# Expert weights in 1 MB units for the first ten experts of each layer instead of the first five

## The chip, the cores and the metric

The kernel runs on one core of a Trainium2 chip. The time is device microseconds (us) of one execution. Five engines work side by side: PE (matrix products), DVE (vector), ACT (scalar), POOL and SP; SP's queue only issues DMA transfers here. Before the change three runs took 1260.52 to 1263.24 us, median 1263.21 us. The execution that was profiled took 1264.12 us.

## The reference

Two layers on 256 tokens of width 1024, in float32. Layer 0 mixes the tokens by forgetting attention (phase A), layer 1 by retention (phase C). After each mixer a router picks one of 4 groups for a token and 2 of its 8 experts, and each expert is a SwiGLU product:

```python
def expert_block(args):
    xb, e = args
    a, b = jnp.split(xb @ w_gu[e], 2, axis=-1)
    return (jax.nn.silu(a) * b) @ w_down[e]
...
h = x
for i in range(DEPTH):
    hn = rms_norm(h, norm_mix[i])
    h = h + mixer(hn)             # attention in layer 0, retention in layer 1
    hn = rms_norm(h, norm_ffn[i])
    h = h + hier_moe(hn, ...)     # 32 experts
return rms_norm(h, norm_final)
```

(`mixer` stands for the two calls.) All 32 experts of a layer get tokens, so all weights are read: an expert has `w_gu` of 1024 x 1024 (4 MB) and `w_down` of 512 x 1024 (2 MB), 192 MB in a layer.

## The kernel before, in words

**The order of work.** Phase A, the expert phase of layer 0, phase C, the expert phase of layer 1, the last norm. An expert phase goes through experts 0 to 31 in order, in groups of four. For an expert, PE multiplies its tokens with `w_gu` (`first_product`, line 1047), ACT and DVE make the SwiGLU product, DVE transposes it, and PE multiplies it with `w_down` (`expert`, line 1075). After the third expert of a group PE gathers the tokens of the next group (`gather`, line 970), after the fourth it scatters the results (line 1101). After the first group comes `overflow`, a loop under an `If` for experts with more than 32 tokens (line 1254); with these inputs it is jumped over, but every engine has to pass the branch in its own order.

**The weights.** All weights go through one list, `Stream.todo`, in the order in which PE uses them, into 26 units of SBUF of 1 MB each (`NSLOT`). A transfer of 1 MB takes one free unit, `one()`; a transfer of 2 MB takes a free pair of neighbours, units 2i and 2i + 1, `two()`. `done` gives units back when the last product that reads them has been written down, and `pump` then issues what is next in the list. `pump` never passes over an item: when the first item finds no pair, it stops there.

```python
            slot = self.one() if units == 1 else self.two()
            if slot is None:
                return
...
    def pieces(e):
        return 2 if e < FINE or e == NE - 1 else 1
```

`pieces` (line 282) tells how an expert is cut. With 1 piece there are three transfers of 2 MB, two for `w_gu` and one for `w_down`; with 2 pieces there are six of 1 MB. `first_product` and `expert` call `done` as soon as a transfer's own products are issued: after 8 matmuls of line 1047 for 1 MB of `w_gu` (16 in the profile), after 16 for 2 MB. `FINE` is thus the number of experts at the start of a layer that come in 1 MB units; expert 31 always does.

**Units that are not weights.** The work buffers take units from the same 26 (`claim`, `Room`): one for the router, two more that are claimed at expert 0, and two that `overflow` claims before its branch and gives back behind it. `reserve` keeps as many units free as are about to be claimed.

**The queue.** Every transfer of the list is issued by SP, in list order (line 166). A DMA waits until PE has read what was in its units. It also waits for the landing of the DMA eight places before it, since there are eight DMA semaphores in turn; so at most eight transfers are under way. Which units a transfer gets, and so which PE product it waits for, is decided when the program is built.

Of the kernel before, what the change touches and what calls it, by code (L numbers as in the profile page):

```python
# [28 lines left out]
CAP = 32  # L29
NSLOT = 26  # L30

FINE = 5
AHEAD = 3

WARM = 29
# [192 lines left out]
def trunk(ctx, tc, x, fox_w_in, fox_b_f, fox_w_out, ret_w_in, ret_gn_gain, ret_w_out,  # L228
# [53 lines left out]
    def pieces(e):  # L282
        return 2 if e < FINE or e == NE - 1 else 1

# [1292 lines left out]
```

## Time and profile before

| what | value |
|---|---|
| runs before | 1260.52, 1263.24, 1263.21 us; median 1263.21 us |
| the profiled execution | 1264.12 us; its span 1262.4 us |
| PE busy | 992.3 us, 79% of the span |
| DVE, ACT, POOL busy | 416.7, 317.0, 46.8 us |
| SP's DMA queue, share of 16 DMA engines | 90.0% |
| read from HBM | 459.70 MB, 365 GB/s over the span |
| mean granted TensorE clock | 0.915 of full speed |

Three views are used. The windows view gives the busy time of each engine and the DMA rate in a stretch; a stretch with a lower rate than its neighbours is one in which the DMA engines had nothing to do for part of the time. The timeline of SP tells when a transfer was issued, and what it cost on SP; the view of DMA issues tells how long after its issue it landed, so that the sum is its time of landing. The timeline of PE has in brackets how long PE stood before an instruction, and what ended that.

### The profile page before, as it was taken

How to read it: one execution, taken by the hardware profiler on the slowest of the kernel's cores; microseconds unless marked ns; L12 is line 12 of the kernel's file. 1: busy time of each engine (PE TensorE's matmuls, PEld its weight loads, DVE VectorE, ACT ScalarE, POOL GpSimd, SP SyncE). 2: the span in 40 equal slices, each digit the busy share in tenths (PEclk: the TensorE clock that was granted, in tenths of full speed). 3: DMA queues.
4: the chain of work that ended last, by engine and by line, in shares of the span. 5: the costliest groups of instructions: out<-in, count | busy, mean ns of one | idle time of the engine just before them, and what ended most of it. 6: DMA issues, size and time to landing. Idle time of an engine off the chain costs nothing. (4 is left out here: it accounts for less than half of the span.)

```text
span 1262.4 us, 21607 instructions
## 1 busy us (share of the span) xinstructions
PE 992.3 (79%) x9279; PEld 638.7 (51%) x9279; DVE 416.7 (33%) x931; ACT 317.0 (25%) x670; POOL 46.8 (4%) x55
## 2 busy tenths in 40 slices
PE   8999986777576666678999999977766666676787
PEld 8888853343232333234989888743432333233344
DVE  6776741211111111112777776421111111111113
ACT  5665521111010010101554665311110101010111
POOL 2000000000000000000223100000000000000001
PEclk9999999999797979789999999999978787877879
DMA  9966878999999999999982678779999999999994
GB/s 327 336 253 228 307 295 342 429 424 428 427 427 427 428 427 426 428 428 393 371 318 77 242 258 336 276 295 421 427 427 426 427 428 428 426 428 426 428 424 175
DMA packets 70088, 462.22 MB, mean 366 GB/s; under 512 B 8401, under 2 KB 13281, under 8 KB 41570
## 3 DMA queue, kind: packets, MB, share of 16 engines
q1 hardware_dynamic: 69568, 460.70, 90.0%
q8 instruction: 75, 1.23, 0.4%
q14 instruction: 27, 0.22, 0.0%
q10 hardware_dynamic: 418, 0.07, 0.0%
HBM read 459.70 MB, written 1.05 MB: 365 GB/s over the span
## 5 line engine op out<-in xcount | busy, mean ns | idle before, releaser
L1047 PE MATMUL sc<-slot,slot 128*32 128x256 f32 x4096 | 281.2, 426 | 57.5 <-DMA slot<-in_expert_w_gu_dram 54.2
L1047 PEld LDWEIGHTS sc<-slot,slot 128*32 128x32 f32 x4096 | 137.8, 120 | 188.4 <-issue 81.3
L1075 PE MATMUL o<-slot,slot 128*32 128x256 f32 x1984 | 145.5, 441 | 105.3 <-DMA slot<-in_expert_w_down_dram 59.6
L1075 PEld LDWEIGHTS o<-slot,slot 128*32 128x32 f32 x1984 | 72.5, 123 | 173.6 <-issue 85.6
L1057 DVE TENSOR_TENSOR slot<-slot,sc 128x128 f32<-128x128 f32 x64 | 23.8, 371 | 396.6 <-ACT slot L1056 396.6
L467 DVE SCALAR_TENSOR_TENSOR slot<-slot,gT,slot 128x512 fp32r<-128x512 f32 x160 | 125.0, 801 | 50.0 <-ACT slot L456 48.6
L500 PE MATMUL acc<-slot,slot 128*128 128x256 f32 x960 | 125.1, 287 | 0.9 <-ACT slot L456 0.4
L1090 DVE COPY slot<-o 32x256 f32<-32x256 f32 x124 | 51.8, 418 | 215.4 <-PE o L1075 188.2
L456 ACT ACTIVATE slot<-slot,gT 128x512 fp32r<-128x512 f32 x160 | 111.4, 718 | 36.2 <-PE acc L500 15.1
L500 PEld LDWEIGHTS acc<-slot,slot 128*128 128x128 f32 x960 | 118.6, 192 | 3.3 <-ACT slot L456 0.7
L1088 ACT ACTIVATE slot<-o 32x256 f32<-32x256 f32 x124 | 46.5, 375 | 292.6 <-DVE slot L1090 292.6
L1056 ACT ACTIVATE slot<-sc 128x128 f32<-128x128 f32 x64 | 17.7, 277 | 383.9 <-PE sc L1047 383.9
L512 PE MATMUL acc<-slot,slot 128*128 128x512 f32 x256 | 102.5, 400 | 0.0
L513 PE MATMUL acc<-slot,slot 128*128 128x512 f32 x256 | 100.1, 391 | 1.8 <-DVE slot L467 1.8
L514 PE MATMUL acc<-slot,slot 128*128 128x512 f32 x256 | 100.1, 391 | 0.0
L970 PE MATMUL sc<-h,slot 128*128 128x512 f32 x112 | 69.3, 778 | 33.5 <-DVE slot L959 33.5
L1101 PE MATMUL acc<-slot,slot 128*128 128x512 f32 (+1 forms) x128 | 60.9, 611 | 13.2 <-ACT slot L1088 13.2
L970 PEld LDWEIGHTS sc<-h,slot 128*128 128x128 f32 x112 | 26.5, 247 | 73.0 <-issue 73.0
L513 PEld LDWEIGHTS acc<-slot,slot 128*128 128x128 f32 x256 | 48.2, 188 | 11.6 <-DVE slot L467 2.7
L514 PEld LDWEIGHTS acc<-slot,slot 128*128 128x128 f32 x256 | 48.1, 188 | 10.2
L512 PEld LDWEIGHTS acc<-slot,slot 128*128 128x128 f32 x256 | 48.2, 188 | 9.3 <-issue 0.3
L978 DVE TENSOR_TENSOR slot<-pt,gT 128x512 f32<-128x512 f32 x28 | 19.4, 692 | 93.1 <-PE pt L977 93.1
(236 smaller groups left out, 763.2 us busy)
## 6 DMA issues: line engine op xcount, KB each, us to landing
slot<-in_expert_w_gu_dram SPq DMA_DIRECT2D x104, 2048.0 KB, 39.1
slot<-in_expert_w_down_dram SPq DMA_DIRECT2D x52, 2048.0 KB, 39.1
slot<-in_expert_w_gu_dram SPq DMA_DIRECT2D x46, 1024.0 KB, 7.5
slot<-in_ret_w_in_dram SPq DMA_DIRECT2D x24, 1024.0 KB, 14.2
slot<-in_expert_w_down_dram SPq DMA_DIRECT2D x20, 1024.0 KB, 7.7
slot<-in_fox_w_in_dram SPq DMA_DIRECT2D x15, 1024.0 KB, 13.3
slot<-in_ret_w_out_dram SPq DMA_DIRECT2D x8, 1024.0 KB, 8.8
slot<-in_fox_w_out_dram SPq DMA_DIRECT2D x4, 1024.0 KB, 15.5
```

The source lines that it names most:

```text
L456: A.activation(wh, w, AF.Copy, scale=1.0 if g is None else g)
L467: V.scalar_tensor_tensor(wl, w, g, wh, ALU.mult, ALU.subtract)
L500: mm(o, w[:, P * j:P * j + P], x[:, k, :], start=first and k == 0 and j % 2 == 0, stop=last and k == 7, skip_group_check=True)
L512: mm(banks[t], xh[:, q], wh, start=first and k == ks[0], stop=False)
L513: mm(banks[t], xh[:, q], wl, start=False, stop=False)
L514: mm(banks[t], xl[:, q], wh, start=False, stop=last and k == ks[-1])
L970: mm(b, o[:, t, :], h[:, t, 512 * n:512 * n + 512], start=t == 0, stop=t == 1)
L1047: mm(bgu[32 * j:32 * j + 32, 0:256].rearrange("p (two f) -> p two f", two=2), xg[:, kk, 32 * e4:32 * e4 + 32], wv[:, :, P * j:P * j + P], ...
L1075: mm(by[32 * nb:32 * nb + 32, 0:256], gTt[:, 32 * j:32 * j + 32], w[:, j % n, 256 * nb:256 * nb + 256], start=j == 0, stop=j == 3, skip_gr ...
L1088: A.activation(o, i, AF.Copy)
L1090: V.tensor_copy(o, i)
L1101: mm(sums[t, n], w2["scm"][0:rows, P * t:P * t + P], y4[0:rows, 512 * n:512 * n + 512], start=start, stop=False, skip_group_check=True)
```

## The change

One constant: the number of experts of a layer whose weights come in 1 MB units goes from five to ten.

```diff
--- before.py
+++ after.py
@@ -29,7 +29,7 @@
 CAP = 32
 NSLOT = 26
 
-FINE = 5
+FINE = 10
 AHEAD = 3
 
 WARM = 29
```

Experts 5 to 9 of both layers are loaded by 60 transfers of 1 MB instead of 30 of 2 MB. The bytes, the list's order and the matmuls are the same. Their units differ from there on, and so do the units that `overflow` borrows.

On SP, in layer 0, the transfers of experts 5 and 6 stood like this (a row is the line, the operation, `unit<-tensor` and its elements; 128x4096 is 2 MB; names of the form `slot_38_1971` are a pair, or a unit, of SBUF), with the load of the branch's number behind them:

```order
L166 DMA slot_38_1971<-in_expert_w_gu_dram 128x4096
L166 DMA slot_39_2047<-in_expert_w_gu_dram 128x4096
L166 DMA slot_40_2057<-in_expert_w_down_dram 128x4096
L166 DMA slot_41_2102<-in_expert_w_gu_dram 128x4096
L166 DMA slot_42_2112<-in_expert_w_gu_dram 128x4096
L166 DMA slot_43_2142<-in_expert_w_down_dram 128x4096
L1200 TENSOR_LOAD nri_1860
```

In the changed kernel the same two experts stand like this (128x2048 is 1 MB):

```order
L166 DMA slot_8_117<-in_expert_w_gu_dram 128x2048
L166 DMA slot_4_100<-in_expert_w_gu_dram 128x2048
L166 DMA slot_5_107<-in_expert_w_gu_dram 128x2048
L166 DMA slot_29_1403<-in_expert_w_gu_dram 128x2048
L166 DMA slot_30_1405<-in_expert_w_down_dram 128x2048
L166 DMA slot_31_1431<-in_expert_w_down_dram 128x2048
L166 DMA slot_16_125<-in_expert_w_gu_dram 128x2048
L166 DMA slot_6_109<-in_expert_w_gu_dram 128x2048
L166 DMA slot_34_1593<-in_expert_w_gu_dram 128x2048
L166 DMA slot_35_1595<-in_expert_w_gu_dram 128x2048
L166 DMA slot_26_440<-in_expert_w_down_dram 128x2048
L166 DMA slot_17_127<-in_expert_w_down_dram 128x2048
```

Six transfers became twelve, each into a single unit; three more, of expert 7, stand between them and the branch.

On PE, the products of expert 5 in layer 0 read these units (x16 counts matmuls in a row):

```order
-L1047 MATMUL sc<-slot_1971,slot_989 32x256 x16
-L1047 MATMUL sc<-slot_2047,slot_989 32x256 x16
-L1075 MATMUL o<-slot_2057,slot_989 32x256 x16
+L1047 MATMUL sc<-slot_117,slot_989 32x256 x8
+L1047 MATMUL sc<-slot_100,slot_989 32x256 x8
+L1047 MATMUL sc<-slot_107,slot_989 32x256 x8
+L1047 MATMUL sc<-slot_1403,slot_989 32x256 x8
+L1075 MATMUL o<-slot_1405,slot_989 32x256 x8
+L1075 MATMUL o<-slot_1431,slot_989 32x256 x8
```

The work is the same; a unit is free after half as many matmuls (one of the program shows as two in the profile).

On SP, behind the branch of layer 0, the list went on before with these rows (in brackets the semaphores that a row waits for; DMAHW are the landings of earlier transfers):

```order
L1254 UNCONDITIONAL_BRANCH
L166 DMA slot_44_2293<-in_expert_w_gu_dram 128x4096 [waits DMAHW5_49,PE_49]
L166 DMA slot_45_2303<-in_expert_w_gu_dram 128x4096 [waits DMAHW6_49,PE_49]
L166 DMA slot_46_2321<-in_expert_w_down_dram 128x4096 [waits DMAHW7_49,PE_49]
L166 DMA slot_47_2335<-in_expert_w_gu_dram 128x4096 [waits DVE_49,DMAHW0_49,PE_49,Activation_49]
```

And in the changed kernel with these:

```order
L1254 UNCONDITIONAL_BRANCH
L166 DMA slot_18_129<-in_expert_w_gu_dram 128x2048 [waits DMASW4_49,DMASW5_49,DMASW3_49,DMASW6_49,DMASW2_49,DMASW7_49,DMASW1_49,DMAHW6_49,DMASW0_49,PE_49]
L166 DMA slot_19_131<-in_expert_w_down_dram 128x2048 [waits DVE_49,DMAHW7_49,PE_49,Activation_49]
L166 DMA slot_37_1771<-in_expert_w_down_dram 128x2048 [waits DMAHW0_49,PE_49]
L166 DMA slot_21_135<-in_expert_w_gu_dram 128x2048 [waits DMAHW1_49,PE_49]
```

The two units that `overflow` borrows are now refilled right behind the branch; those rows wait for the other engines to have passed it, which before only the fourth row did.

## Rows read from the trace of the kernel before

**Rows 1.** Page: the span, and GB/s in 40 equal slices of it.

```profile
span 1262.4 us, 21607 instructions
GB/s 327 336 253 228 307 295 342 429 424 428 427 427 427 428 427 426 428 428 393 371 318 77 242 258 336 276 295 421 427 427 426 427 428 428 426 428 426 428 424 175
```

**Rows 2.** Windows: start:end, width, busy us of each engine, PEclk, DMA share, GB/s.

```profile
230.00:540.00 310.00, 206.35 (x2292) 101.40 (x2284) 49.86 (x120) 32.34 (x85) 0.00 (x0) 0.88 1.01 427
680.00:700.00 20.00, 20.00 (x101) 16.98 (x100) 14.54 (x26) 10.71 (x17) 5.80 (x6) 1.00 0.38 118
```

**Rows 3.** Windows, as rows 2, at the start of both expert phases.

```profile
190.00:200.00 10.00, 6.35 (x68) 3.12 (x61) 2.37 (x6) 1.03 (x3) 0.00 (x0) 0.87 0.75 275
200.00:210.00 10.00, 7.85 (x89) 4.25 (x91) 2.06 (x4) 1.47 (x3) 0.00 (x0) 0.96 0.81 308
840.00:850.00 10.00, 7.28 (x32) 3.76 (x36) 2.58 (x5) 1.83 (x4) 0.00 (x0) 0.83 0.30 126
850.00:860.00 10.00, 7.85 (x95) 3.74 (x86) 1.60 (x5) 1.03 (x3) 0.00 (x0) 1.00 0.86 338
```

**Rows 4.** Timeline of the SP queue: issue time, duration, transfer, count.

```profile
174.30 0.33 SPq L166 DMA_DIRECT2D slot<-in_expert_w_gu_dram  x1
180.01 0.33 SPq L166 DMA_DIRECT2D slot<-in_expert_w_down_dram  x1
211.47 0.33 SPq L166 DMA_DIRECT2D slot<-in_expert_w_down_dram  x1
...
818.03 0.33 SPq L166 DMA_DIRECT2D slot<-in_expert_w_gu_dram  x1
819.76 0.33 SPq L166 DMA_DIRECT2D slot<-in_expert_w_gu_dram  x1
824.61 0.33 SPq L166 DMA_DIRECT2D slot<-in_expert_w_down_dram  x1
850.34 0.33 SPq L166 DMA_DIRECT2D slot<-in_expert_w_down_dram  x1
862.09 0.34 SPq L166 DMA_DIRECT2D slot<-in_expert_w_down_dram  x1
```

**Rows 5.** DMA issues one by one, in rows 4 without 850.34: KB, us to landing.

```profile
slot<-in_expert_w_gu_dram SPq DMA_DIRECT2D x1, 1024.0 KB, 7.4
slot<-in_expert_w_down_dram SPq DMA_DIRECT2D x1, 1024.0 KB, 9.1
slot<-in_expert_w_down_dram SPq DMA_DIRECT2D x1, 2048.0 KB, 13.8
slot<-in_expert_w_gu_dram SPq DMA_DIRECT2D x1, 1024.0 KB, 5.4
slot<-in_expert_w_gu_dram SPq DMA_DIRECT2D x1, 1024.0 KB, 9.4
slot<-in_expert_w_down_dram SPq DMA_DIRECT2D x1, 1024.0 KB, 9.5
slot<-in_expert_w_down_dram SPq DMA_DIRECT2D x1, 2048.0 KB, 11.7
```

**Rows 6.** Timeline of PE after experts 2, 3 and 7: start, duration, idle before.

```profile
204.60 3.66 PE L1047 MATMUL sc<-slot,slot 128*32 128x256 f32 x64
220.19 2.18 PE L1047 MATMUL sc<-slot,slot 128*32 128x256 f32 x28 [2.76 <-issue]
...
849.21 3.66 PE L1047 MATMUL sc<-slot,slot 128*32 128x256 f32 x64
860.97 3.66 PE L1047 MATMUL sc<-slot,slot 128*32 128x256 f32 x64 [0.30 <-PEq L1254]
898.18 1.93 PE L1075 MATMUL o<-slot,slot 128*32 128x256 f32 x32 [1.21 <-DVE slot L1064]
```

**Rows 7.** Timeline of PE near the end of each expert phase.

```profile
580.91 1.07 PE L1075 MATMUL o<-slot,slot 128*32 128x256 f32 x16 [1.63 <-DMA slot<-in_expert_w_down_dram]
...
1204.88 1.93 PE L1047 MATMUL sc<-slot,slot 128*32 128x256 f32 x16 [2.84 <-DMA slot<-in_expert_w_gu_dram]
```

## The prediction

> **What bounds the kernel now.** I read the page's line of GB/s first [rows 1]. For most of both expert phases it stands at 421 to 429: slices 8 to 18 and 28 to 39, each 31.6 us wide. Nothing in the trace moves weights faster for long, so there the kernel is as long as its bytes: 427 GB/s over 310 us [rows 2] make 1.0486 MB / 427 = 2.46 us for a unit of 1 MB and 14.7 us for an expert. PE confirms it at the end of each phase, where what it waits for is a DMA [rows 7]. Lower rates stand ahead of these, and slices 6, 7, 26 and 27 are where the expert phases start (295, 342, 276 and 295). Phase C itself is PE's: busy 20.00 of 20.00 us at 118 GB/s [rows 2]; what DMA could do there changes nothing.
>
> So a microsecond in which the DMA engines stand idle inside an expert phase is a microsecond of the kernel, and I looked for those in windows of 10 us at the start of both phases. The first 10 us or so, in which PE routes and all units are full, can't be filled. But behind them the rate is 275 and 308 GB/s in layer 0, and 126 and 338 in layer 1 [rows 3], with PE at work and units coming free. Against 427 that is (152 + 119) x 10 us = 2.7 MB and (301 + 89) x 10 us = 3.9 MB not moved, 6.3 and 9.1 us.
>
> The timeline of SP says why. In layer 1 the transfer of expert 5's `w_down` (2 MB) goes out only at 850.34, right after PE has begun expert 3 at 849.21 [rows 4, 6]. By the program it needs a pair; one half is free early, the other is the first unit of expert 3. Until then six single units and more lie free, and the list doesn't pass over an item that finds no pair.
>
> **The change part by part.** *Removed: the waits for pairs of experts 5 and 6.* With 1 MB transfers each unit that PE gives back is refilled at once. I measure by landings (issue plus time to landing). In layer 0 the last 1 MB transfer that is the same in both kernels, expert 4's last, lands at 180.01 + 9.1 = 189.1, and expert 6's last at 211.47 + 13.8 = 225.3 [rows 4, 5]: 36.2 us for 12 MB. In layer 1 it is 824.61 + 9.5 = 834.1 and 862.09 + 11.7 = 873.8: 39.7 us. In the changed kernel these 24 MB take 24 p, where p is the pace of 1 MB transfers that land behind one another.
>
> *Added: that pace for experts 7 to 9 too.* Their 36 MB in both layers go at p instead of 2.46 us, as they lie in the saturated stretch. The gain is 36.2 + 39.7 - 24 p - 36 (p - 2.46) = 164.5 - 60 p.
>
> *The pace.* In layer 0 the second of the last five 1 MB transfers lands at 174.30 + 7.4 = 181.7, the fifth at 189.1: 7.4 / 3 = 2.47 us. In layer 1 the first lands at 818.03 + 5.4 = 823.4, the third at 819.76 + 9.4 = 829.2, the fifth at 834.1: 2.9 us each for two steps, then 2.45 for two [rows 4, 5]. The two slow steps follow an empty queue, the other five steps a filled one, and the new transfers have a filled one before them. The bounds are 2.45 (gain 17.5) and 2.9 (loss 9.5); I take 2.47, the row nearest to the case: 16.3 us, 6.4 + 9.9 less 36 x 0.01.
>
> *Does the queue stay filled?* PE gives back 18 units in experts 0 to 2, of which two go to work buffers, so 16 transfers can go before PE begins expert 3 at 204.60 and 849.21 [rows 6]. In layer 0 the first of them lands at 181.7 - 2.47 = 179.2, the 16th at 179.2 + 15 x 2.47 = 216.3; in layer 1 the 16th is at 834.1 + 11 x 2.47 = 861.3. The next transfer takes expert 3's first unit, which came free by 850.34, and a transfer into an idle queue lands after 5.4 us: 855.7, and 206 + 5.4 = 211 in layer 0. Both are covered, by some 5 us. Four more follow from expert 3, to 226.1 and 871.2. Then comes the branch: the next two requests wait until the engines have passed it. PE passes at 860.97 after 0.30 us, and so 866.4 is early enough in layer 1; in layer 0 PE stands another 2.76 us inside its first product behind the branch, until 220.19 [rows 6], and 220.8 + 5.4 = 226.2 is no cover at all if the borrowed units come as late as that. I take 1 us off for it: 15.3 us. SP itself has nine more rows ahead of the branch, but PE doesn't wait for SP there, and SP comes to it when expert 3's units are issued, before PE.
>
> *Issuing 30 more DMAs* costs SP 0.33 us each [rows 4], 10 us in all, against 2.47 us that each takes to land; it is hidden while eight are under way, that is 20 us of work. Without that cover it would be the 5.4 us of a lone transfer.
>
> *Does it reach the end?* All later work hangs on the stream: PE waits for it until 580.91 in layer 0 and 1204.88 in layer 1, and runs on without it from there [rows 7]. Phase C is PE's alone and starts earlier by what layer 0 saves.
>
> The profiled execution took 1264.1 us, so the changed one takes 1248.8. The median of the three runs is 0.9 us under the profiled one: 1247.9.
>
> **A rule that speaks against it.** A lone 1 MB transfer takes 5.4 us, three behind one another 2.47 each [rows 5]. The Trainium skill, in *DMA: Bandwidth & Descriptors*, section "Anatomy of one DMA — SWDGE (gpsimd) path", gives a DMA a fixed part of about 2.0 us beside its bytes at 436 GB/s. If each request paid that in turn, 30 more would cost 60 us by the page and the change would lose 43 us; with transfers under way together, as the steps of 2.47 us show, it is paid in the queue's shadow, and the sum stays at 15.3.
>
> **The rivals.**
> 1. *The slow pace holds (slower).* If the 2.9 us of the two steps in layer 1 were the pace of a queue with eight 1 MB transfers under way instead of eight of 2 MB, the gain would be 164.5 - 60 x 2.9 = -9.5: 1273. It turns at p = 2.74. For it: those two steps. Against it: the five others. 5%.
> 2. *Every request pays its fixed share (slower).* 5.4 - 2.46 = 2.9 us for each of 30 more requests is 88 us, less the 16.9 of the closed gaps: 1334. The steps of 2.47 us exclude it as far as they reach. 1%.
> 3. *The gap moves to experts 10 to 12 (no change).* There the transfers are pairs again, and free units have other neighbours; if the same waits came back, 1263 to 1265. For it: the last of expert 10's transfers takes a pair of units of expert 7. Against it: PE is through with expert 7's last product at 898.18 + 1.93 = 900.1 [rows 6], and by then the stream has work up to 834.1 + 30 x 2.47 + 4 x 2.46 = 918. Some 12 us of cover remain above the 5.4 us of a landing. 6%.
> 4. *Layer 0's part is lost (smaller gain).* If the branch in layer 0 leaves the queue empty for longer, or phase C doesn't pass the shift on, 9.9 less 0.2 is left: 1253.5. For it: the bare cover. Against it: PE's wait at 580.91. 10%.
>
> **How the numbers follow.** My forecast has 78%, rival 4 10%, rival 3 6%, rivals 1 and 2 together 6%. A measurement of this kernel tells 0.3% (3.8 us) from no change. Faster by more: forecast and rival 4, 88%. Within it: rival 3 and a little of rival 1 with a pace near 2.74, 7%. Slower: 5%. The forecast's own range is 1246.7 (2.45 us) to 1252 (2.54). The range for 8 in 10 reaches over rival 4 and one microsecond of run-to-run spread: 1244.5 to 1255.
>
> **What would show each step.** In the changed profile the windows 190 to 210 and some 840 to 860 us should be at 420 GB/s or more. The landing of expert 6's last transfer should be at about 219 in layer 0, 6.4 us earlier, and in layer 1, which begins some 5 us earlier, at 16 us earlier than 873.8. 1 MB transfers should land 2.47 us apart, and no window between 250 and 300 us should fall below 420. A window below 400 behind 226 us would mean the branch or the pairs of expert 10; steps of 2.7 us or more, rival 1; a layer 0 that ends earlier and a phase C that doesn't begin earlier, rival 4.

## The result and the profile after

The changed kernel takes 1250.39 us (median of 4 runs, 1249.70 to 1251.18) beside 1263.22 us for the kernel before (4 runs, 1260.52 to 1263.68). The ratio is 0.9903, with a 95% interval of 0.9886 to 0.9920: 12.8 us faster, where 15.3 were forecast. The profiled execution took 1251.18 us, 12.9 less than the one before.

The page of the changed kernel, span and GB/s in 40 equal slices of 31.2 us:

```profile
span 1249.4 us, 21664 instructions
GB/s 337 340 249 217 316 287 420 421 426 428 426 426 428 426 428 426 429 426 385 378 308 68 260 245 301 339 359 420 422 427 426 429 427 426 428 427 428 428 423 186
```

Slice 7, at 342 before [rows 1], is at 420, and slices 26 and 27, at 276 and 295 before, are at 339 and 359. What the change aimed at is thus visible on the page. The windows show it in place (start:end, width, busy us of each engine, granted clock, DMA share, GB/s):

```profile
190.00:200.00 10.00, 6.35 (x57) 3.10 (x50) 2.37 (x6) 1.62 (x4) 0.00 (x0) 1.00 1.01 420
200.00:210.00 10.00, 6.90 (x106) 3.94 (x105) 2.64 (x6) 1.25 (x3) 0.00 (x0) 1.00 1.02 422
250.00:300.00 50.00, 37.74 (x474) 19.44 (x470) 9.64 (x24) 5.96 (x16) 0.00 (x0) 0.93 1.01 426
300.00:560.00 260.00, 172.94 (x1856) 84.17 (x1846) 37.97 (x92) 24.80 (x66) 0.00 (x0) 0.86 1.01 427
840.00:850.00 10.00, 8.46 (x56) 4.58 (x60) 1.81 (x3) 1.19 (x2) 0.00 (x0) 0.83 1.01 420
850.00:860.00 10.00, 7.55 (x80) 3.26 (x76) 1.52 (x4) 1.02 (x3) 0.00 (x0) 1.00 1.02 424
```

275, 308, 126 and 338 GB/s [rows 3] have become 420 to 424, and behind them, up to the last weights of each phase, no window of 10 us falls below 412. The queue of SP in the changed kernel: issue time, duration, transfer, count. The `w_down` rows at 204.11 and 849.06 are the last transfer of expert 6, in layer 0 and in layer 1, those at 535.69 and 1178.22 the last of expert 30; the two rows at 213.70 and 214.53 go into the units that stand behind the branch.

```profile
204.11 0.33 SPq L166 DMA_DIRECT2D slot<-in_expert_w_down_dram  x1
213.70 0.34 SPq L166 DMA_DIRECT2D slot<-in_expert_w_gu_dram  x1
214.53 0.33 SPq L166 DMA_DIRECT2D slot<-in_expert_w_down_dram  x1
535.69 0.33 SPq L166 DMA_DIRECT2D slot<-in_expert_w_down_dram  x1
849.06 0.33 SPq L166 DMA_DIRECT2D slot<-in_expert_w_down_dram  x1
1178.22 0.33 SPq L166 DMA_DIRECT2D slot<-in_expert_w_down_dram  x1
```

How long five of them took to land (KB, us from issue to landing), in the same order without 214.53:

```profile
slot<-in_expert_w_down_dram SPq DMA_DIRECT2D x1, 1024.0 KB, 14.7
slot<-in_expert_w_gu_dram SPq DMA_DIRECT2D x1, 1024.0 KB, 15.0
slot<-in_expert_w_down_dram SPq DMA_DIRECT2D x1, 2048.0 KB, 40.7
slot<-in_expert_w_down_dram SPq DMA_DIRECT2D x1, 1024.0 KB, 12.0
slot<-in_expert_w_down_dram SPq DMA_DIRECT2D x1, 2048.0 KB, 40.3
```

Expert 6 is complete at 218.8 in layer 0 (225.3 before) and at 861.1 in layer 1 (873.8 before) [rows 4, 5]: 6.5 and 12.7 us earlier, where 6.4 and 16 were forecast. The last transfer of expert 30 lands at 576.3 and 1218.5; before it was 580.8 and 1229.3. So layer 0 keeps 4.4 of its 6.5 us, and the timeline of TensorE shows that still less goes on from there (start, duration, idle before and what ended it):

```profile
213.87 1.06 PE L1047 MATMUL sc<-slot,slot 128*32 128x256 f32 x14 [0.30 <-PEq L1254]
217.45 3.21 PE L1047 MATMUL sc<-slot,slot 128*32 128x256 f32 x50 [2.51 <-issue]
...
576.48 1.07 PE L1075 MATMUL o<-slot,slot 128*32 128x256 f32 x16 [2.59 <-DMA slot<-in_expert_w_down_dram]
577.48 1.17 PE L533 MATMUL sc<-ones 128*128 128x128 f32 x4
578.57 1.94 PE L1075 MATMUL o<-slot,slot 128*32 128x256 f32 x16
580.44 2.75 PE L533 MATMUL sc<-ones 128*128 128x128 f32 x20
...
598.70 1.57 PE L500 MATMUL acc<-slot,slot 128*128 128x256 f32 x8
...
814.03 3.66 PE L1047 MATMUL sc<-slot,slot 128*32 128x256 f32 x64
...
1219.66 1.07 PE L1075 MATMUL o<-slot,slot 128*32 128x256 f32 x16 [0.57 <-DVE slot L1064]
```

The wait that ends at 576.48 is 4.4 us earlier than its counterpart at 580.91 [rows 7]. But sixteen matmuls that take 1.07 us take 1.94 just behind it: after those 2.59 us without a matmul, and one group at full speed, TensorE runs at its lower level (1.2 GHz, not 2.4). From 577 to 583 us its granted clock is 0.72, and these rows cost 1.6 us more than at the full clock. Phase C begins at 598.70 instead of 601.55, 2.85 us earlier, and layer 1 at 814.03 instead of 816.90.

### The profile page after: what moved, and what is told of

Read it like the earlier page. It is cut to its first block, busy times and chain, and to the rows that moved or that the text cites. A ratio compares the mean times of both kernels' runs of the same rounds, so it can differ in the third digit from the quotient of the medians.

```text
span 1249.4 us, 21664 instructions
## 1 busy us (share of the span) xinstructions
PE 978.7 (78%) x9279; PEld 634.9 (51%) x9279; DVE 415.8 (33%) x931; ACT 317.1 (25%) x670; POOL 46.7 (4%) x55
## 5 line engine op out<-in xcount | busy, mean ns | idle before, releaser
L1047 PE MATMUL sc<-slot,slot 128*32 128x256 f32 x4096 | 273.2, 417 | 59.7 <-DMA slot<-in_expert_w_gu_dram 56.6
L1075 PE MATMUL o<-slot,slot 128*32 128x256 f32 x1984 | 139.5, 426 | 103.4 <-DMA slot<-in_expert_w_down_dram 53.9
L970 PE MATMUL sc<-h,slot 128*128 128x512 f32 x112 | 72.6, 810 | 33.5 <-DVE slot L959 33.5
```

Source lines behind the costliest of these rows:

```text
L970: mm(b, o[:, t, :], h[:, t, 512 * n:512 * n + 512], start=t == 0, stop=t == 1)
L1047: mm(bgu[32 * j:32 * j + 32, 0:256].rearrange("p (two f) -> p two f", two=2), xg[:, kk, 32 * e4:32 * e4 + 32], wv[:, :, P * j:P * j + P], ...
L1075: mm(by[32 * nb:32 * nb + 32, 0:256], gTt[:, 32 * j:32 * j + 32], w[:, j % n, 256 * nb:256 * nb + 256], start=j == 0, stop=j == 3, skip_gr ...
```

## The experiments

The theory: the gain is the closing of the two stretches in which the list stands still, because its head wants a pair of units and one half of it comes late. Against it stood that smaller requests help by themselves, that the wait moves to the next pair, and that one layer carries the gain. All times are medians.

**One layer alone.** `pieces` gets the layer and uses 10 in layer 1 only:

```
-        return 2 if e < FINE or e == NE - 1 else 1
+        return 2 if e < (FINE if l else 5) or e == NE - 1 else 1
```

> The first ten experts in 1 MB pieces in layer 1 only, the first five in layer 0 as before. Theory (the gain is the waits for pairs that go, each layer by itself): layer 0's landings as before, layer 1's expert 6 nearly 10 us earlier, so 1253 to 1254; layer 0's part of the changed kernel's gain is then the rest, 3 us. Rival (layer 0's shift is what counts, or one layer's change spoils the other): 1250 or 1258 and more.

Measured 1254.76 us beside 1263.81, ratio 0.9928 (0.9915 to 0.9941). Its windows, one in layer 0 and one in layer 1:

```profile
190.00:200.00 10.00, 6.35 (x72) 3.17 (x65) 2.37 (x6) 1.02 (x3) 0.00 (x0) 0.89 0.75 288
840.00:850.00 10.00, 6.94 (x24) 3.51 (x28) 2.43 (x6) 1.94 (x4) 0.00 (x0) 0.83 1.02 423
```

The hole in layer 0 is there, that in layer 1 is gone; the time is 0.8 us above the range that was expected. 9.1 us belong to layer 1; to layer 0 the rest of the changed kernel's gain: 12.8 - 9.1 = 3.7 us, or 2.5 by the second measurement of the changed kernel (1252.20 beside 1263.78, below). The profile says 2.85.

**Small requests, but still in pairs.** Experts 5 to 9 of the kernel before, with each 2 MB loaded by two requests into a pair that is taken and given back whole:

```
-                       cut=2 if (e, i) == (NE - 1, 3) else 1)
+                       cut=2 if (e, i) == (NE - 1, 3) or FINE <= e < 10 else 1)
...
-                    st.add(("wd", l, e, i), wd[:, c * i:c * i + c, :], c)
+                    st.add(("wd", l, e, i), wd[:, c * i:c * i + c, :], c, cut=2 if FINE <= e < 10 else 1)
```

> Experts 5 to 9 still take a free pair of units and give it back as a pair, as before, but each pair is loaded by two requests of 1 MB. Theory (the wait for a pair is the cause): the empty stretches at 190 to 210 and 840 to 860 us stay, and 60 MB at 2.48 instead of 2.44 us per MB cost up to 2 us: 1262 to 1266. Rival (the size of the request is the cause, because PE can begin on the first MB and a unit lands sooner): the stretches fill and the time is 1250 to 1253.

Measured 1264.25, ratio 1.0004 (0.9994 to 1.0015): no gain. Its windows:

```profile
190.00:200.00 10.00, 6.35 (x83) 3.32 (x76) 2.37 (x6) 1.02 (x3) 0.00 (x0) 0.92 0.60 220
200.00:210.00 10.00, 7.85 (x87) 4.36 (x89) 2.06 (x4) 1.47 (x3) 0.00 (x0) 1.00 0.97 378
840.00:850.00 10.00, 6.66 (x26) 3.04 (x19) 2.38 (x5) 1.94 (x4) 0.00 (x0) 0.83 0.41 170
850.00:860.00 10.00, 7.85 (x105) 4.00 (x105) 2.21 (x5) 1.03 (x3) 0.00 (x0) 1.00 0.75 287
```

With the same small requests and the wait for the pair the holes stay: against 427 GB/s 2.6 MB are missing in layer 0 and 4.0 MB in layer 1, in the kernel before 2.7 and 3.9. The size of the request is not the cause.

**No small requests, but other pairs.** The kernel before, in which a 2 MB transfer may take any two neighbouring units:

```
         for i, u in enumerate(self.free):
-            if u ^ 1 in list(self.free)[:i]:
...
+            for v in (u ^ 1, u + 1 if u % 2 else u - 1):
+                if v in list(self.free)[:i]:
+                    self.free.remove(u)
+                    self.free.remove(v)
+                    return min(u, v)
```

> The kernel before (the first five experts in 1 MB pieces), but a 2 MB transfer may take any two neighbouring units, not only an even one and the odd one after it. No request is smaller than before. Theory (what counts is that free units without a free partner hold the list up): the same stretches fill, 4.9 of 6.1 us in layer 0 and 9.8 of 10.1 in layer 1, so 1249 to 1252. Rival (the 1 MB requests themselves bring the gain, by landing sooner): no gain, 1262 to 1265.

Measured 1251.01, ratio 0.9901 (0.9884 to 0.9919), the changed kernel's gain without a single added request. Its windows, and the issue of expert 5's `w_down` in layer 1, which went out at 850.34 before [rows 4] (line 166 is 167 here):

```profile
190.00:200.00 10.00, 6.35 (x71) 3.03 (x64) 2.37 (x6) 1.03 (x3) 0.00 (x0) 0.84 0.95 377
200.00:210.00 10.00, 8.39 (x79) 4.44 (x77) 1.61 (x3) 1.47 (x3) 0.00 (x0) 0.91 0.91 356
840.00:850.00 10.00, 9.05 (x79) 4.72 (x77) 1.38 (x2) 1.19 (x2) 0.00 (x0) 0.83 1.02 416
...
831.96 0.33 SPq L167 DMA_DIRECT2D slot<-in_expert_w_down_dram  x1
```

The same request of 2 MB goes out 18 us earlier, long before TensorE begins expert 3 (846.64 here) and not just behind it; in the kernel with small requests in pairs it stayed at 851.53. The hole of layer 1 is closed. That of layer 0 is closed only in part (1.2 MB of the 2.7 are still missing, less filled than expected), since one transfer of expert 6 goes out at 207.67 as it did before (207.46); on the other hand no expert pays the pace of 1 MB steps. The two experiments together settle it: small requests that still wait for a pair bring nothing, and requests of the old size that needn't wait for an aligned pair bring the changed kernel's time. Nor is it that a unit comes free after half as many matmuls, for here each pair is given back whole.

**How many experts.** The constant alone, `FINE = 6`, `7` and `32`:

> The first six experts in 1 MB pieces. Theory (the wait belongs to a certain pair, and is as long as that pair's second half comes late): layer 0 is cured, but in layer 1 expert 6's w_down now waits for the first unit of expert 3 as expert 5's did, from 6 MB later, so 6 to 7 us of the 10 come back: 1255 to 1258. Rival (one more expert in small pieces is enough): 1250 to 1252. Rival (nothing short of 7 helps): 1260 or more.

> Only experts 5 and 6 join those in 1 MB pieces, the first seven. Theory: the waits that go are those of experts 5 and 6, so nearly the whole gain is there, 1249 to 1253, if the first pairs, those of experts 7 and 8, find their two halves free in time; the place to look is behind expert 6's last transfer, 835 to 880 us. Rival (the wait moves to the first pair wherever it stands): as long as before, 1260 or more, with an empty stretch of 5 to 10 us there in layer 1.

> All experts in 1 MB pieces. Theory (the gap is closed once and 1 MB steps are slower by 0.035 us each than half a 2 MB step): 252 MB more at 2.48 instead of 2.445 us, 8.8 us, so 1257 to 1260. Rival (smaller units keep buffers fresher and PE's waits shorter, the more the better): 1250 or less. Rival (each request has a fixed cost): far above 1263.

The last two columns give the landing of expert 30's last transfer in each layer, by issue plus time to landing; the rows for 5 and 10 are the profiled kernels before and after. Each ratio is to runs of the kernel before on the same chip; the medians come from several chips.

| first experts in 1 MB | median us | ratio (95%) | layer 0 | layer 1 |
|---|---|---|---|---|
| 5 | 1263.22 | 1 | 580.8 | 1229.3 |
| 6 | 1256.38 | 0.9938 (0.9922 to 0.9954) | 575.7 | 1223.1 |
| 7 | 1252.24 | 0.9912 (0.9896 to 0.9928) | 576.3 | 1218.3 |
| 10 | 1250.39 | 0.9903 (0.9886 to 0.9920) | 576.3 | 1218.5 |
| 32 | 1256.76 | 0.9946 (0.9933 to 0.9960) | 581.5 | 1225.1 |

With 6 the wait moves one expert on in layer 1, at the price that the late half had let expect (window of that kernel):

```profile
850.00:860.00 10.00, 8.06 (x88) 4.10 (x91) 1.44 (x4) 0.75 (x2) 0.00 (x0) 1.00 0.50 179
```

With 7 only a dent is left at the same place:

```profile
850.00:860.00 10.00, 8.76 (x100) 4.60 (x104) 0.84 (x2) 0.75 (x2) 0.00 (x0) 1.00 0.95 367
```

With 32 the price of the small steps shows, in the middle of layer 0:

```profile
300.00:560.00 260.00, 178.86 (x1848) 78.47 (x1840) 37.98 (x92) 24.80 (x66) 0.00 (x0) 0.82 1.01 420
```

420 GB/s against 427 in the same window of the changed kernel: 1.0486 MB / 420 = 2.497 us for a MB instead of 2.456. It issues 390 requests for expert weights, the changed kernel 264. In the stream the 126 more cost 0.08 us each: expert 30's last landing in layer 0 is 5.2 us later, for 63 of them. Of the 10 us that this would make in both layers the time shows 4 to 5.4 (ratio 0.9946 against 0.9914 and 0.9903), a little less than expected. Part of it comes back at the end of layer 1: TensorE begins expert 30's `w_down` at 1223.36, before its second MB lands at 1225.1, so the matmuls behind the expert (line 1113) are 3.9 us later than in the changed kernel while the landing is 6.6 us later.

The Trainium skill (*DMA: Bandwidth & Descriptors*, "Anatomy of one DMA — SWDGE (gpsimd) path") gives a fixed part of about 2.0 us for each DMA of the gpsimd path; if each of the 126 paid that in turn, an estimate by that page is 252 us. These runs, on SP's queue with up to eight requests under way, show nothing of the kind; a DMA of the gpsimd path was not run.

**Both cures at once.** `FINE = 7` and the other pairs:

> The first seven experts in 1 MB pieces, and 2 MB transfers on any two neighbouring units. Theory: no wait for a pair is left in either layer, and three experts fewer go at the 1 MB pace, 18 MB in each layer at 0.035 us: 1 us better than the changed kernel, 1249 to 1250.5. Rival (the pace of 1 MB steps doesn't matter or other steps set the end): 1250.5 to 1252.

Measured 1251.63, ratio 0.9904 (0.9887 to 0.9921). Its windows have no hole (425 GB/s from 850 to 860 us), but the last microsecond that I expected did not come, and that theory fell.

**Where layer 0's part went.** In the last experts the kernel runs matmuls on constants (`keep_warm`), from `WARM` on. `WARM = 27`, `24` and `31` (none in experts 29 and 30, only those after expert 30's products) in the changed kernel, the changed kernel once more beside them, and `WARM = 27` with `FINE = 8`:

> The changed kernel, with the matmuls that keep TensorE busy begun at expert 27 instead of 29. Theory (in layer 0 part of what the stream gains is lost again as TensorE falls to its lower clock in a wait for expert 30's weights, 1.6 us in the profiled run): earlier dummy matmuls don't reach into that wait, so no difference, 1250 to 1252. Rival (they hold the clock): 1248 to 1249.5. Rival (they make TensorE late): 1252 or more.

> The changed kernel once more, beside its variants. Theory: 1249 to 1252, and the stream in layer 1 again without an empty stretch.

> The changed kernel without the matmuls that keep TensorE busy in experts 29 and 30 (those from expert 30's end on stay). Theory (TensorE's lower clock after its last waits for weights takes part of the gain away, since what follows the last weights hangs on TensorE): 2 to 6 us slower than the changed kernel. Rival (the transfers alone set the end): no difference within 1 us.

> The changed kernel with those matmuls from expert 24 on. Theory (what they are worth is that TensorE comes to the last waits with its clock high; expert 27 is early enough, where the wait for expert 30's weights was passed without a fall): as with 27, 0.5 to 2 us faster than the changed kernel. Rival (the difference that 27 made was the spread between runs): equal to the changed kernel, 1250 to 1251.

> The first eight experts in 1 MB pieces and TensorE kept busy from expert 27 on. Theory: no wait for a pair is left with eight (four 2 MB units of cover less than with ten), 12 MB in each layer go at 2.44 instead of 2.48, 0.8 us; with the held clock together 1 to 2.5 us faster than the changed kernel, 1248 to 1249.5. Rival (a pair of expert 8 waits in layer 1): 1251 or more, with an empty stretch near 865.

| kernel | median us (runs) | ratio (95%) |
|---|---|---|
| changed, again | 1252.20 (1250.93 to 1254.38) | 0.9914 (0.9896 to 0.9932) |
| `WARM` 27 | 1249.45 (1249.06 to 1249.78) | 0.9885 (0.9866 to 0.9905) |
| `WARM` 24 | 1250.14 (1248.71 to 1251.14) | 0.9896 (0.9879 to 0.9913) |
| `WARM` 31 | 1249.42 (1246.72 to 1250.44) | 0.9887 (0.9869 to 0.9905) |
| 8 experts, `WARM` 27 | 1248.64 (1247.74 to 1251.12) | 0.9887 (0.9869 to 0.9904) |

In the profile with 27 the full clock is held at the end of layer 0, as the rival said and not my theory: the timeline of TensorE has the times of the full clock behind the same wait, and no 1.94.

```profile
576.02 1.07 PE L1075 MATMUL o<-slot,slot 128*32 128x256 f32 x16 [1.64 <-DMA slot<-in_expert_w_down_dram]
577.02 0.71 PE L533 MATMUL sc<-ones 128*128 128x128 f32 x4
577.66 1.07 PE L1075 MATMUL o<-slot,slot 128*32 128x256 f32 x16
```

Yet the second profile of the changed kernel has no fall there either (granted clock 1.00 from 577 to 583 us, after waits of 2.70 and 1.66 us), so the fall doesn't come in every execution. And leaving these matmuls out, which should have cost 2 to 6 us, gained 2.8; none of the six runs reaches into those of the changed kernel. That theory fell. The end of layer 1 shows what stands against it. The changed kernel again, expert 30's `w_down`, landed at 1217.3:

```profile
1220.21 1.07 PE L1075 MATMUL o<-slot,slot 128*32 128x256 f32 x16 [0.57 <-DVE slot L1064]
```

The kernel with `WARM = 31`, the same, landed at 1217.3 as well:

```profile
1217.47 3.49 PE L1075 MATMUL o<-slot,slot 128*32 128x256 f32 x32 [2.37 <-DMA slot<-in_expert_w_down_dram]
```

Without them TensorE runs at the lower clock, but it is there when the weights land and even waits 2.37 us; with them it comes 2.9 us late. From there to the matmuls behind the expert (line 1113, at 1225.18 and 1222.90) it takes 5.4 us at the lower clock instead of 5.0, so 2.3 of the 2.7 us between the two starts are kept: the profiled span is 1247.7 beside 1250.0.

But more of these matmuls help as well, and at the same place. With `WARM = 27` the same weights landed at 1217.2:

```profile
1217.75 1.07 PE L1075 MATMUL o<-slot,slot 128*32 128x256 f32 x16 [0.57 <-DVE slot L1064]
```

TensorE is 0.5 us late there instead of 2.9. It does the same dummy matmuls in experts 29 and 30, but its granted clock from 1210 to 1215 us is 0.67, and 0.50 in the changed kernel's second profile (in its first it is 0.75, and TensorE 1.2 us late). So what the dummy matmuls cost at the end hung on the clock at which they ran; leaving them out and beginning them earlier both bring TensorE to the last weights nearer to their landing. This rests on one profile of each kernel.

`WARM = 27` alone was timed on another chip than the four others, beside 1264.61 us. Measured again, the changed kernel came out 0.2 us above its expected range. `WARM = 24` was 2.1 us under the changed kernel, about as expected. The last kernel has the lowest median of all, 3.6 us under the changed kernel on the same chip. Its runs and those of the changed kernel just touch (1251.12 and 1250.93), and against `WARM = 31` it isn't resolved. The three ways to 1249 stand as equals.

## Why the prediction was right, and by how much it missed

**What bounds the kernel.** Right. All nine measurements of kernels that closed layer 1's hole whole or nearly and layer 0's at least in good part, with at most ten experts in small pieces, lie at 1248.6 to 1252.2, and the one kernel that kept both stayed at 1264.

**The removed waits.** The sum writes "6.4 + 9.9 less 36 x 0.01", but 6.4 and 9.9 have the pace taken off already; 16.3 is right. The term is right in layer 1: from the phase's start (814.03 for 816.90) expert 6 is complete 9.9 us earlier, as forecast. In layer 0 the first product is 0.8 us earlier in this execution, ahead of anything that the change touches; 5.7 us are left of the 6.4, and two 1 MB steps there took 5.90 us instead of 4.96. In the second profile of the changed kernel the 12 MB land in 29.8 us, 6.3 us less than before.

**The pace.** 2.48 us, forecast 2.47. For experts 7 to 9 I had charged 0.36 us in both layers; from expert 6's last landing to expert 9's it is 44.65 and 44.88 us instead of 44.18 and 44.03, 1.3 us. The price is small, but it is the difference to the 2 MB pace that counts, and that was 0.04 and not 0.01 us per MB.

**The cover at the branch.** The 1 us taken off wasn't needed. TensorE did stand for 2.51 us (2.76 before [rows 6]), but SP had issued into the borrowed units at 213.70, before TensorE went on at 217.45; the request took 15.0 us to land since others lay ahead of it, and landings go on at steps of 2.48 us. The queue stayed filled, as the landing sum said.

**Thirty more requests** are hidden, as forecast. Rivals 1 and 2 are gone with the pace, and rival 3 (the gap moves on) with 426 GB/s from 250 to 300 us; with 6 experts it would have come true. Gone too is the rule that spoke against the change; it was taken from a section on the gpsimd path, and these transfers are SP's.

**It reaches the end: this is the step that failed in part**, in layer 0. Its term was worth 5.4 us with all deductions, and 2.85 arrived. By landings: 6.5 us earlier at expert 6, 6.0 at expert 9, 4.4 at expert 30. Between the last two lies one long step more than before (the list of them is below), 1.6 us. Then TensorE's lower clock behind its last wait took 1.6. I had let the shift through with the words that all later work hangs on the stream; the stream's own disturbances and TensorE's clock behind the last landing were no terms of the sum. Rival 4 had the place right, but it lost the whole of layer 0's part and not half of it.

**Layer 1** brought its 9.9, lost 0.8 in the pace and 1.1 more behind expert 9, and got 1.8 back: TensorE took expert 30's last weights 1.2 us after they landed (1219.66), before 3.0 us after. With the 2.85 of layer 0 and 0.4 behind the last matmul that makes the 13.0 by which the span shrank.

How much of these last terms is the kernel and how much the single execution is partly open: the second profile of the changed kernel starts phase C 4.1 us earlier than the kernel before and then comes 2.9 us late to the last weights.

## What to carry to other kernels

When a transfer must wait for two particular buffers, look at what else is free in that moment: here, by the prediction's count, six and more single units lay idle behind an item at the head of the list that found no pair, and either smaller items or a freer choice of pairs brought the same gain (ratios 0.9903 and 0.9901). Make the items small only where the wait is; the small pace was paid for everywhere else (32 experts: 4 to 5.4 us back). And when the stream comes earlier, see who is last at its end: work that was put there to fill a wait can make its engine late when the wait shrinks.

## What the runs showed of the hardware

- In a filled queue the 2 MB steps bring 427 GB/s and the 1 MB steps 420, both for 260 us, with at most eight transfers under way and the DMA share at 1.01.
- Every so often one or two neighbouring landings come late together by 1.0 to 1.6 us while the windows stay near 427. In layer 1 of the changed kernel they end at 926.69, 1060.48 and 1203.90 us (6.09, 6.21 and 6.16 us for a 2 MB step of 4.89), in layer 0 of the kernel before at 319.87 and 482.75 (6.44 and 6.30): 134 to 163 us apart. In layer 0 of the changed kernel there are three (273 to 289, 417 to 428, 565 to 576 us). What makes them wasn't tried and stays open.
- TensorE's clock can fall just behind a wait, and not only in it: the first sixteen matmuls of line 1075 after 2.59 us without any took 1.07 us, the next sixteen 1.94. It doesn't always: in the second profile the sixteen matmuls after 2.70 us without any took 1.07 us, and so did the next sixteen.
